# Conditioning rows loaded first, twelve tiles for modulation weights, and layer 0's five later modulation pieces on TensorE

## The chip, the core and the metric

The kernel runs on one core of a Trainium2 chip (trn2). The core has five instruction queues that run at the same time and wait for each other through semaphores: TensorE (PE in the profile; its weight loads are a row of their own, PEld), VectorE (DVE), ScalarE (ACT), GpSimd (POOL) and SyncE (SP), which issues nearly all the DMAs of this kernel. The metric is device microseconds of one execution. The kernel before took 1816.23 us (median of three runs, 1811.3 to 1817.52).

## The reference, cut to what matters

Two layers of a transformer trunk over 512 latent tokens and 256 context tokens, width 1024, all in float32. Every layer is modulated: a matrix product of the conditioning vector with `w_ada` gives six rows of 1024 numbers (shift, scale and gate for the attention half, the same for the FFN half), once for the latent tokens (`c`) and once for the context tokens (`c_ctx`).

```python
silu_c, silu_cc = silu(c), silu(c_ctx)
for l in range(2):
    mod   = silu_c  @ w_ada[l] + b_ada[l]        # (1024) @ (1024, 6*1024)
    mod_c = silu_cc @ w_ada[l] + b_ada[l]
    sh_a, sc_a, gt_a, sh_f, sc_f, gt_f = split(mod, 6)      # the same for mod_c
    h  = rms(x,  g_attn_pre) * (1 + sc_a)  + sh_a
    hc = rms(xc, g_attn_pre) * (1 + csc_a) + csh_a
    # one input projection for three head groups (MLA, differential, GQA)
    q, k, v of each group = project(h @ w_in[l]), project(hc @ w_in[l])
    x  = x  + gt_a  * rms(attention(...) @ w_out[l], g_attn_post)
    xc = xc + cgt_a * rms(...)                                # layer 0 only
    hf = rms(x, g_ffn_pre) * (1 + sc_f) + sh_f
    x  = x + gt_f * rms((silu(hf @ w_gate) * (hf @ w_up)) @ w_down, g_ffn_post)
    # and the same for xc in layer 0
```

## The kernel before

The work is cut into stages, each of which is a `Plan`: a list of steps, and for each step the engines that may do it with an estimated duration on each, the steps that it follows, the buffers that it takes, and a rank. When the kernel is built, `Plan.schedule` plays the list through: whenever an engine is free it takes the ready step with the lowest rank, and a step that several engines may do goes to the one that would end it first. The order that comes out is what each engine's queue holds; on the chip an engine runs its queue in that order and waits, in order, for whatever the next instruction needs. So every duration in the plan and every rank can move the order of all five queues.

The stages are, for the first layer: a start stage (the `with` block from line 839, tiles from pool `e0`), the rest of the input projection (from line 1003, which this text calls the projection stage), the attention, and then three plans for the output projection, the FFN's two first products and the down projection; the second layer has the same but for the start, which the first layer's last plan does for it.

Matrix products of the trunk are taken as three products of float32r parts (`mm3`, lines 433 to 437): a high part `wh` (cast by ACT at line 490) and a low part `wl` (the rest, line 431, on DVE or POOL) of each weight tile, and the same of the activations.

`ada` (line 504) computes one piece of the modulation: 512 of the 1024 columns of one of the six rows `v`. It loads eight tiles of `w_ada`, 128 by 512 each (256 KB), through a ring of tiles (`st` in the start stage, 7 of them; `ast` in the projection stage, 3 of them). There are three ways:

- `rows` and `columns`: DVE multiplies each tile by its column of `silu(c)` and adds it up (lines 527 and 529), once for each of the two streams (latent, context); then the sum is split into a high and a low part (`pair`) and TensorE adds up its 128 partitions. In `rows` two matmuls of 512 columns for each stream do that (line 545), and the row goes to DRAM (`mod_d`). In `columns` eight small matmuls for each stream do it (line 550) and leave the result in columns, where it is used.
- `pe`: TensorE multiplies each tile directly (line 519: 128 by 2 stationary, 512 float32 columns moving), eight matmuls for both streams at once, a copy and four small transposes (line 580) turn the row into columns.

In the start stage four pieces of layer 0 are done, two by `columns` and two by `pe` (`S_WAY`), and a fifth (`S_LATER`) by `rows`. In layer 0's projection stage the five pieces of `W_LATER[0]` are all done by `rows`, and so are the four pieces of `W_LATER[1]` in layer 1's, for one stream only. `mod_columns` (line 602) reads the FFN half's rows back from DRAM and turns them into columns (line 609). The conditioning vectors are loaded by `load_c` (lines 852, 853) into `crow`, turned by TensorE (line 856) and put through Silu by ACT (line 857) into `sc`, on which all of `ada` waits. `row_columns` loads the biases and gains (lines 629, 631).

`lean` is a flag of a plan: steps that DVE may do are then not offered to POOL. It is off in the projection stages. `KIND` chooses between two sets of estimated durations; set 1 is in force from layer 0's output projection to its down projection, and likewise in layer 1.

Of the kernel before, what the change touches and what calls it, by code (L numbers as in the profile page):

```python
# [59 lines left out]
D_ADA = (-2.8, 12, 15, 18.06, 27.82, 38)  # L60
W_ORDER = (('a', 'gq', 'v'), ('a', 'gq', 'v'))
W_MLA = (2, 2)
W_QB = (-23.02, 10.44)
W_MR = (30.2, 40.9)
W_ROPE = (23.16, -12.09)
W_GQN = (35.45, 8.86)
W_ADA = (-2.51, -2)
W_ADA_STEP = (3.15, 8)
W_BIAS = (1.57, 3.22)
R_KP = (41.16, 51.47)  # L70
O_BIAS = (0.99, 0.19)
O_Y = (((-23.8, -14.51), (-23.14, -6.37)), ((-23.71, -25.03), (-22.35, 6.93)))
O_FIN = (-1.05, -20.02)
O_W = (1.59, -10.71)
O_TAIL = ((1, 7), (1, 6))
O_GATE = (19.45, -11.16)
O_CH = ((13.48, 16.45), (9.41, 21.58))
O_CHS = (0.65, -3.01)
O_MOD = (-0.24, -11.23)
O_TR = (-3.5, -25.57)  # L80
O_W0 = (16.11, -1.02)
O_W1 = (36.25, 12)
F_BIAS = (0.27, 0.5)
F_ADA = (6.19, 0)
F_ADA_STEP = 4.5
F_W = (-11.64, -5.09)
# [7 lines left out]
D_CHS = (4.07, 1)  # L94
# [14 lines left out]
S_ROW = 0.4  # L109
S_CH = (149.71, 128.84, 43.28, -19.45)  # L110
# [25 lines left out]
class Plan:  # L136
# [7 lines left out]
    wrote, read, free, gone, over = {}, {}, {}, {}, 0.0  # L144

    @classmethod
    def reset(cls):
        cls.wrote, cls.read, cls.free, cls.gone, cls.over = {}, {}, {}, {}, 0.0
# [12 lines left out]
    def add(self, rank, ways, emit, after=(), takes=(), uses=(), lag=None, reads=(), writes=(), room=None):  # L161
# [3 lines left out]
        s = SimpleNamespace(rank=rank, n=len(self.steps), ways=ways, emit=emit, takes=takes, uses=(*takes, *uses),  # L165
# [51 lines left out]
    def schedule(self):  # L217
# [34 lines left out]
        while len(order) < len(self.steps):  # L252
            t = heapq.heappop(events)
            more = True
            while more:
                more = False
                for e in ready:
# [3 lines left out]
                    while ready[e]:  # L261
# [4 lines left out]
                        if s.at <= t and e == min(s.ways, key=lambda o: max(free[o], t) + s.ways[o] + (  # L266
                                self.bias if o == "dve" else 0)) and self.fits(s, t):
                            free[e] = t + s.ways[e]
                            self.start(s, free[e], e)
# [29 lines left out]
DMA = 0.66  # L299
# [6 lines left out]
KIND = [0]  # L306

# [40 lines left out]
def _body(nc, tc, es, I, out):  # L348
# [155 lines left out]
    def ada(plan, rank, l, v, c0, nstr, tiles, way="rows", late=False):  # L504
# [7 lines left out]
        for k in range(NK):  # L512
# [5 lines left out]
            if by_pe:  # L518
                last[0] = plan.add(rk, {"pe": 4 * c_mm(512) + 0.2}, lambda _, k=k, st=st: mm(
                    ps.tile[:2, :], lhsT=sc[:, :, k], rhs=st.tile[:, :512], start=(k == 0), stop=(k == NK - 1)),  # L520
                    [x, last.get(0, [])], [] if k else [ps], [st, ps] if k else [st], reads=["sc"])
                continue
            for s, a in enumerate(acc):
                def mac(_, s=s, a=a, k=k, st=st):
# [3 lines left out]
                    else:  # L528
# [3 lines left out]
                                   [] if k else [a], [st, a] if k else [st], reads=["sc"])  # L532
# [122 lines left out]
    def mean_inv(plan, rank, after, box):  # L655
# [5 lines left out]
        return plan.add(rank, {"pool": 0.46}, lambda _: power(box), [x])  # L661
# [79 lines left out]
    def residual(plan, rank, t, ps, gate, stage, dst, X, junk, after, mt_of):  # L741
# [12 lines left out]
        r = plan.add(rank, {"pool": 0.46}, lambda _: power(box), [plan.add(rank, {"dve": 0.13}, mean, a)])  # L754
# [84 lines left out]
    with ExitStack() as s0:  # L839
# [3 lines left out]
        plan = Plan({"m": 8, "st0": 7, "acc0": 4, "row0": 2, "pair": 1, "x": 6, "mt": 6, **RING}, ("m", "st0", "acc0", "row0"), 0.3)  # L843
        tiles = (held("st0", e0, [128, 512], 7), held("acc0", e0, [128, 512], 4), held("row0", e0, [128, 512], 2),
# [10 lines left out]
        x = plan.add(-50, {"sp": 2 * DMA}, load_c, lag=2.2)  # L855
        x = plan.add(-50, {"pe": 0.1}, lambda _: nc.tensor.transpose(psc.tile[:, 0:16], crow, ident[:16, :16]), [x], [psc])
        plan.add(-50, {"act": 1.5}, lambda _: A.activation(
# [12 lines left out]
        for i, (v, c0) in enumerate(S_LATER):  # L870
            ada(plan, 100 + i, 0, v, c0, 2, tiles)
# [3 lines left out]
    for l in range(DEPTH):  # L875
# [6 lines left out]
        with ExitStack() as sa:  # L882
# [50 lines left out]
            def rms_heads(rank, x, H, g, t, after, key):  # L933
# [20 lines left out]
                y = plan.add(rank, {"dve": c_vec(n) + 0.07}, sums, [y], (), [tmp])  # L954
                y = plan.add(rank, {"pool": 0.3 + 0.16 * H}, power, [y])
# [46 lines left out]

            sw = ExitStack()
# [4 lines left out]
            plan = Plan({"m": 8, "P": P_BUFS - nw - (1 if nw else 0), "qk": 4, "OT": 3, "sm": 2, "ast": 3, "pair": nw, **RING}, ("m", "P", "ast", "sm", "pair"), W_BIAS[l])  # L1008
# [1038 lines left out]
```

## Time and profile before

| | |
|---|---|
| median of three runs | 1816.23 us (1811.3 to 1817.52) |
| the profiled execution's own time | 1813.22 us |
| its span, first to last instruction | 1811.4 us |
| mean granted TensorE clock | 0.976 |
| instructions | 27865 |
| start stage, to the first matmul of part `a` | 0 to 94.7 us |
| layer 0's projection stage, to the first attention score | 94.7 to 235.8 us |

The profile is one execution. Its page gives busy time by engine and a picture in 40 slices; the trace behind it can be asked for groups of instructions by line, for who waited for whom, for the chain of work that ended last, for the timeline of one engine, and for the busy time of each engine in a stretch. Busy times of PE are modelled at their ends (a matmul of 512 columns is shown as 0.39 us and the next one starts 0.23 us after it), so the spacing of the starts is what a matmul costs when others follow it.

### The profile page before, as it was taken

The page shows a single profiled execution, that of the slowest core. Times are in us where ns is not written, and L with a number is a line of the kernel's source. Part 1 is how long each engine was busy: PE and PEld are TensorE (multiplying, and loading weights), DVE is VectorE, ACT ScalarE, POOL GpSimd, SP SyncE. Part 2 cuts the span into 40 slices and gives each one's busy share as a digit, 9 for nine tenths or more (in the row PEclk, how much of TensorE's full clock was granted, in tenths as well). Part 3 has the DMA queues.
Part 4 walks back from the last instruction along what each step waited for, and adds up shares of the span by engine and source line. Part 5 has one row for each costly group of instructions (what it writes and reads, how often), then busy time and mean ns, then how long its engine had stood idle before and what let it go on. Part 6 is the DMA issues. An engine that isn't in the chain of part 4 may idle for free.

```text
span 1811.4 us, 27865 instructions
## 1 busy us (share of the span) xinstructions
PE 1696.4 (94%) x9906; PEld 1494.3 (82%) x9906; DVE 1381.5 (76%) x1981; ACT 989.7 (55%) x2035; POOL 731.3 (40%) x789
## 2 busy tenths in 40 slices
PE   6888799999999999999999998988999979999998
PEld 2676588798888999999777888777898879999886
DVE  5869878887669899976788645558898799988444
ACT  3344278998586444443346564447996754555212
POOL 3576967788100000000000027886875127444212
PEclk8899899999999999999999999989999989999999
DMA  8245103100664544522888635402003644332532
GB/s 293 80 153 163 52 14 82 25 1 29 243 183 132 168 128 151 156 93 89 290 283 256 210 95 179 159 14 66 23 2 117 213 132 123 105 104 71 174 100 75
DMA packets 152636, 227.80 MB, mean 126 GB/s; under 512 B 14473, under 2 KB 86121, under 8 KB 152497
## 3 DMA queue, kind: packets, MB, share of 16 engines
q1 hardware_dynamic: 152496, 226.02, 39.4%
q8 instruction: 78, 1.28, 0.3%
q14 instruction: 62, 0.50, 0.1%
HBM read 197.58 MB, written 18.17 MB: 119 GB/s over the span
## 4 chain that ended last, share of the span: by engine, by line
PE 53%; DVE 14%; DMA 9%; ACT 9%; POOL 8%; issue 7%; SPq 0%; DVEq 0%; ACTq 0%; POOLq 0%
PE m L1742 25%; PE m L436 5%; PE m L435 5%; PE m L437 5%; PE s L1410 4%; DVE wl L431 3%; DMA st<-in_w_ffn_down 2%; PE m L1384 2%; PE m L1527 2%; DMA st<-in_w_out 2%; PE m L1468 2%; DVE P L529 2%; ACT wh L490 2%; ACT P L1423 1%; DMA st<-in_w_ada 1%
## 5 line engine op out<-in xcount | busy, mean ns | idle before, releaser
L1742 PE MATMUL m<-Y,wh 128*128 128x384 f32 (+1 forms) x1408 | 310.2, 311 | 6.0 <-ACT Y L419 4.9
L653 POOL TENSOR_TENSOR r<-v,mhalf 128x1 f32<-128x1 f32 x42 | 29.0, 692 | 687.4 <-DVE v L752 590.8
L490 ACT CAST wh<-st 128x1024 fp32r<-128x1024 f32 (+2 forms) x146 | 151.2, 1037 | 245.6 <-PE m L437 94.8
L431 DVE TENSOR_TENSOR wl<-st,wh 128x1024 fp32r<-128x1024 f32 (+1 forms) x124 | 164.5, 1327 | 107.8 <-ACT wh L490 107.2
L1742 PEld LDWEIGHTS m<-Y,wh 128*128 128x128 f32 x1408 | 239.4, 192 | 7.6 <-ACT Y L419 5.4
L1742 PE MATMUL m<-hT,wh 128*128 128x384 f32 (+1 forms) x1056 | 232.2, 311 | 3.6 <-ACT wh L490 3.6
L1742 PE MATMUL m<-Y,wl 128*128 128x384 f32 (+1 forms) x704 | 219.5, 312 | 6.5 <-DVE wl L431 6.5
L1742 PEld LDWEIGHTS m<-hT,wh 128*128 128x128 f32 x1056 | 178.6, 191 | 5.2 <-ACT wh L490 4.3
L1423 ACT ACTIVATE P<-s,nm 128x768 f32<-128x768 f32 (+1 forms) x200 | 164.4, 826 | 32.1 <-DVE nm L1416 12.5
L1416 DVE TENSOR_REDUCE nm<-s 128x1 f32<-128x768 f32 x160 | 151.1, 950 | 27.6 <-PE s L1410 23.2
L1742 PE MATMUL m<-hT,wl 128*128 128x384 f32 (+1 forms) x528 | 164.3, 311 | 2.3 <-DVE wl L431 2.3
L1692 ACT CAST wh<-X 128x1024 fp32r<-128x1024 f32 x82 | 86.2, 1053 | 113.2 <-PE m L1742 49.7
L435 PE MATMUL m<-wh,hT 128*128 128x512 f32 (+2 forms) x368 | 143.6, 390 | 0.6 <-POOL hT L417 0.4
L436 PE MATMUL m<-wl,hT 128*128 128x512 f32 (+2 forms) x368 | 141.5, 384 | 2.4 <-DVE wl L431 1.6
L437 PE MATMUL m<-wh,hT 128*128 128x512 f32 (+2 forms) x368 | 141.4, 384 | 2.2 <-POOL hT L431 1.7
L1742 PEld LDWEIGHTS m<-Y,wl 128*128 128x128 f32 x704 | 135.1, 192 | 7.9 <-DVE wl L431 7.9
L431 DVE TENSOR_TENSOR wl<-X,wh 128x1024 fp32r<-128x1024 f32 x82 | 107.3, 1309 | 14.2 <-ACT wh L1692 13.6
L436 PE MATMUL m<-wl,nr 128*128 128x512 f32 x264 | 103.4, 392 | 2.1 <-DVE wl L431 2.1
L435 PE MATMUL m<-wh,nr 128*128 128x512 f32 x264 | 103.8, 393 | 0.2 <-ACT wh L490 0.2
L1742 PEld LDWEIGHTS m<-hT,wl 128*128 128x128 f32 x528 | 100.8, 191 | 3.4 <-DVE wl L431 3.4
L437 PE MATMUL m<-wh,nr 128*128 128x512 f32 x264 | 103.0, 390 | 0.0
L529 DVE SCALAR_TENSOR_TENSOR P<-ast,sc,P 128x512 f32<-128x512 f32 x98 | 89.1, 949 | 15.5 <-DMA ast<-in_w_ada 15.2
(333 smaller groups left out, 4364.2 us busy)
## 6 DMA issues: line engine op xcount, KB each, us to landing
st<-in_w_ffn_down SPq DMA_DIRECT2D x66, 512.0 KB
st<-in_w_ada SPq DMA_DIRECT2D x88, 256.0 KB
ast<-in_w_ada SPq DMA_DIRECT2D x72, 256.0 KB
st<-in_w_out SPq DMA_DIRECT2D x32, 512.0 KB
X<-in_w_ffn_gate SPq DMA_DIRECT2D x22, 512.0 KB
X<-in_w_ffn_up SPq DMA_DIRECT2D x22, 512.0 KB
x<-in_w_ffn_up SPq DMA_DIRECT2D x22, 512.0 KB
x<-in_w_ffn_gate SPq DMA_DIRECT2D x22, 512.0 KB
```

The costliest lines, as they stand in the source:

```text
L431: by(e).tensor_tensor(out=out, in0=src, in1=h.bitcast(F32), op=ALU.subtract)
L435: mm(ps, lhsT=a[0], rhs=b[0], start=start, stop=False)
L436: mm(ps, lhsT=a[0], rhs=b[1], start=False, stop=False)
L437: mm(ps, lhsT=a[1], rhs=b[0], start=False, stop=stop)
L490: a = plan.add(rank, {"act": c_act(W) + 0.05}, lambda _: A.copy(out=part(0)[:, :W], in_=st.tile[:, :W]), [x], kept[:1], [st])
L529: V.scalar_tensor_tensor(out=a.tile[:, :512], in0=st.tile[:, :512], scalar=c, in1=a.tile[:, :512], op0=ALU.mult, op1=ALU.add)
L1384: mm(m.tile[0:64, :w], lhsT=U.vt(k + 6 - nk), rhs=kept.tile[:, k * w:(k + 1) * w], start=(k == 0), stop=(k == nk - 1))
L1410: mm(S.tile[:, o], lhsT=q[:, qt * 128:(qt + 1) * 128], rhs=k[:, ks], start=(i == 0), stop=(i == n))
L1416: V.tensor_reduce(out=nm[:, 0:1], in_=S.tile[:, :768], axis=AX.X, op=ALU.max, negate=True)
L1423: A.activation(out=P.tile[:, c], in_=S.tile[:, c], func=AF.Exp, bias=box["nm"][:, i:i + 1], scale=1.0, accum_out=r_()[:, t + i:t + i + 1])
L1692: a = plan.add(rank, {"act": c_act(1024) + 0.05}, lambda _: A.copy(out=kept[0].tile, in_=x.tile), after, kept[:1], [x])
L1742: mm(m.tile[:, :n], lhsT=ww, rhs=moving[y](z, k), start=bool(first) and k == 0 and t == 0, stop=k == 3 and t == 2, skip_group_check=not first)
```

## The change

The two conditioning rows get rank -200 in place of -50 and `row_columns` (`S_ROW`) -147.64 in place of 0.4, so SP issues them before all else. The start stage has 12 tiles for `w_ada` in place of 7. In layer 0's projection stage the five pieces are done by `pe` (`W_WAY[0]`), and the plan is lean; in layer 1's the four pieces are done by `columns`. `mod_columns` is no longer called in either. `KIND` is 1 in layer 0's projection stage too, with some estimated durations changed there (`either`), and a matmul of the `pe` way is planned at 0.45 us in place of 1.06 under set 1. Where set 1 is in force, the schedule lengthens a step on DVE and one on POOL by their overlap if they share operands' ports by a rule written into `add` (`shared`). Many ranks are new: most of the start stage's, some of the projection stage of layer 0, the output projections, the FFN of layer 1 and the down projection of layer 0.

```diff
-S_RANK = 4.71
-S_ADA = (-89.37, -104.7, -63.8, -23.26)
-S_W = (4.4, 70.86, -34.09, 21.27)
-S_X = (-23.02, -119.78, -29.53, 10.12, 31.11, 79.28)
-S_H = (21.12, 71.5, -0.39, 57.38, 59.34, 107.98)
+S_RANK = 18.42
+S_ADA = (-89.37, -93.77, -63.25, 11.71)
+S_W = (4.4, 57.56, -70.74, 21.27)
+S_X = (-40.27, -135.33, -29.53, 18.16, 31.11, 79.28)
+S_H = (21.12, 83.75, 31.93, 57.38, 59.34, 107.98)
...
+W_WAY = (('pe', 'pe', 'pe', 'pe', 'pe'), ('columns', 'columns', 'columns', 'columns'))
+W_LEAN = (True, False)
...
-W_ADA_STEP = (3.15, 8)
+W_ADA_STEP = (3.37, 8)
...
-O_W1 = (36.25, 12)
+O_W1 = (40.29, 17.37)
...
-F_W = (-11.64, -5.09)
+F_W = (-11.64, -21.22)
...
-D_CHS = (4.07, 1)
+D_CHS = (1.37, 1)
...
-S_ROW = 0.4
-S_CH = (149.71, 128.84, 43.28, -19.45)
+S_ROW = -147.64
+S_CH = (149.71, 128.84, 43.28, 7.44)
...
+        shared = shared or ("pool" in ways and ways["pool"] > 1.5 * ways.get("dve", 0.0))
...
+                            o = self.busy.get("pool" if e == "dve" else "dve")
+                            if KIND[0] and e in ("dve", "pool") and o is not None and o.end > t and (
+                                    s.shared or e == "pool") and (o.shared or o.on == "pool"):
+
+                                both = min(s.ways[e], o.end - t)
+                                free[e] += both
+                                o.end += both
...
+def either(a, b):
+    return (a, b)[KIND[0]]
...
-                last[0] = plan.add(rk, {"pe": 4 * c_mm(512) + 0.2}, lambda _, k=k, st=st: mm(
+                last[0] = plan.add(rk, {"pe": either(4 * c_mm(512) + 0.2, 0.45)}, lambda _, k=k, st=st: mm(
...
-        plan = Plan({"m": 8, "st0": 7, "acc0": 4, "row0": 2, "pair": 1, "x": 6, "mt": 6, **RING}, ("m", "st0", "acc0", "row0"), 0.3)
+        plan = Plan({"m": 8, "st0": 12, "acc0": 4, "row0": 2, "pair": 1, "x": 6, "mt": 6, **RING}, ("m", "st0", "acc0", "row0"), 0.3)
...
-        x = plan.add(-50, {"sp": 2 * DMA}, load_c, lag=2.2)
+        x = plan.add(-200, {"sp": 2 * DMA}, load_c, lag=2.2)
...
+            KIND[0] = 1 - l
...
                 for i, (v, c0) in enumerate(W_LATER[l]):
-                    ada(plan, W_ADA[l] + W_ADA_STEP[l] * i, l, v, c0, 2 - l, tiles)
-                mod_columns(plan, W_ADA[l] + W_ADA_STEP[l] * len(W_LATER[l]), l, 1, 2 - l, tiles[2])
+                    ada(plan, W_ADA[l] + W_ADA_STEP[l] * i, l, v, c0, 2 - l, tiles, W_WAY[l][i])
```

## Rows read from the trace of the kernel before

**Rows 1.** The profile page: busy time of each engine over the span, and the slices of PE.

```profile
PE 1696.4 (94%) x9906; PEld 1494.3 (82%) x9906; DVE 1381.5 (76%) x1981; ACT 989.7 (55%) x2035; POOL 731.3 (40%) x789
...
PE   6888799999999999999999998988999979999998
```

**Rows 2.** Busy time by stretch: start and end in us, its length, then for PE, PEld, DVE, ACT and POOL the busy time and the instructions, then the granted clock, the mean share of the DMA engines and GB/s. The first row is the whole projection stage of layer 0, the other two are holes in it.

```profile
94.70:235.80 141.10, 119.63 (x544) 97.38 (x543) 111.83 (x176) 54.64 (x143) 110.72 (x110) 0.94 0.39 119
123.00:129.90 6.90, 1.26 (x5) 0.39 (x4) 4.86 (x13) 4.98 (x20) 6.39 (x13) 0.75 0.46 133
197.40:207.40 10.00, 2.43 (x8) 1.26 (x9) 7.76 (x9) 2.81 (x4) 10.00 (x9) 0.71 0.26 79
```

**Rows 3.** Who waited for whom, PE alone, in the projection stage (94.7 to 235.8 us): us in total, times, the longest.

```profile
PE m L545 <- ACT pair L419: 8.0, 2, 4.5
PE m L545 <- POOL pair L431: 5.5, 4, 2.5
PE m L985 <- DVE ckTl L431: 2.4, 2, 1.7
PE m L545 <- DVE Vm L431: 1.5, 1, 1.5
PE m L985 <- ACT N L424: 1.4, 1, 1.4
PE m L609 <- DVE mql L971: 0.9, 1, 0.9
```

**Rows 4.** Timelines of PE and PEld: start in us, length, engine, line, operation, tiles, count, and the idle time before it. The weight loads of line 519 are shown because each starts when the matmul before it does.

```profile
31.53 1.05 PE L550 MATMUL m<-selr,pair 128*128 128x2 f32 x8
...
32.95 0.09 PEld L519 LDWEIGHTS m<-st,sc 128*2 128x2 f32 x1 [0.34 <-issue]
33.38 0.09 PEld L519 LDWEIGHTS m<-st,sc 128*2 128x2 f32 x1 [0.34 <-issue]
...
39.57 0.41 PE L580 MATMUL m<-ident,row 2*128 2x2 f32 x4 [0.92 <-ACT row L419]
...
129.88 0.63 PE L435 MATMUL m<-wh,hT 128*128 128x512 f32 x1
130.31 0.63 PE L436 MATMUL m<-wl,hT 128*128 128x512 f32 x1
...
137.44 0.39 PE L435 MATMUL m<-wh,hT 128*128 128x512 f32 x1
137.67 0.39 PE L436 MATMUL m<-wl,hT 128*128 128x512 f32 x1
```

**Rows 5.** Groups of instructions by line from 92 to 235 us, of PE, DVE and POOL: line, engine, operation, tiles, count, then busy us, mean ns of one, idle time before them and what ended it.

```profile
L545 PE MATMUL m<-pair,selr 128*2 128x512 f32 x20 | 8.6, 482 | 15.0 <-ACT pair L419 8.0 <-POOL pair L431 5.5 <-DVE Vm L431 1.5
...
L529 DVE SCALAR_TENSOR_TENSOR P<-ast,sc,P 128x512 f32<-128x512 f32 x70 | 59.4, 904 | 4.1 <-DMA ast<-in_w_ada 4.1
L431 DVE TENSOR_TENSOR wl<-st,wh 128x832 fp32r<-128x832 f32 (+1 forms) x5 | 6.1, 1225 | 3.5 <-ACT wh L490 3.4
L527 DVE TENSOR_SCALAR P<-ast,sc 128x512 f32<-128x512 f32 x10 | 5.8, 607 | 2.0 <-POOL pair L431 1.4 <-POOL kpn L916 0.6
...
L431 POOL TENSOR_TENSOR wl<-st,wh 128x1024 fp32r<-128x1024 f32 (+2 forms) x9 | 21.3, 2373 | 13.9 <-ACT wh L490 8.3 <-DMA ast<-in_w_ada 5.6
L431 POOL TENSOR_TENSOR pair<-P,pair 128x512 fp32r<-128x512 f32 x10 | 14.9, 1509 | 6.8 <-ACT pair L419 6.8
L951 POOL TENSOR_TENSOR r<-v,mhalf 128x8 f32<-128x8 f32 (+1 forms) x8 | 12.1, 1517 | 2.7 <-DVE v L946 2.7
```

**Rows 6.** Timeline of SP's queue at the start: what it issues, when, and for how long.

```profile
0.72 3.23 SPq L515 DMA_DIRECT2D st<-in_w_ada  x7
3.99 0.38 SPq L852 DMA_DIRECT2D crow<-in_c  x1
...
7.70 0.33 SPq L629 DMA_DIRECT2D row<-in_b_ada  x1
...
9.03 0.28 SPq L631 DMA_DIRECT2D row<-in_g_ffn_pre  x1
```

**Rows 7.** The chain of work that ended last, in order of time: start in us, length, what. Pieces of the start and, of the projection stage, two waits for a tile of `w_ada`.

```profile
4.41 5.00 DMA crow<-in_c_ctx
...
10.03 4.64 PE m L519 x6
...
142.19 2.90 DMA ast<-in_w_ada
...
198.94 3.48 DMA ast<-in_w_ada
```

**Rows 8.** Busy time by stretch, columns as in rows 2, in the start stage.

```profile
0.00:10.00 10.00, 0.26 (x1) 0.18 (x1) 0.49 (x6) 1.47 (x2) 0.68 (x6) 1.00 0.82 280
10.00:15.00 5.00, 4.97 (x8) 0.85 (x9) 1.34 (x5) 3.45 (x6) 3.00 (x5) 1.00 0.56 194
25.00:50.00 25.00, 21.98 (x74) 10.75 (x74) 23.01 (x35) 9.60 (x25) 12.00 (x10) 0.74 0.93 313
50.00:75.00 25.00, 20.93 (x81) 16.31 (x82) 23.87 (x28) 12.52 (x24) 13.72 (x9) 0.80 0.29 87
```

**Rows 9.** Groups of PE from 1060 to 1200 us, layer 1's projection stage.

```profile
L545 PE MATMUL m<-pair,selr 128*2 128x512 f32 x8 | 3.3, 452 | 3.5 <-POOL pair L431 2.3 <-ACT pair L419 1.2
```

**Rows 10.** Who waited for whom, PE alone, from 1380 to 1540 us: layer 1's output projection and the start of its FFN.

```profile
PE m L1742 <- DVE wl L431: 7.8, 10, 3.0
```

More of the change, by code (lines that the diff above doesn't have):

```diff
@@ L142 @@
     LAG = {"pe": 0.2, "act": 0.14, "dve": 0.13, "pool": 0.07, "sp": 0.15}
-    wrote, read, free, gone, over = {}, {}, {}, {}, 0.0
+    wrote, read, free, gone, over, busy = {}, {}, {}, {}, 0.0, {}
     @classmethod
     def reset(cls):
-        cls.wrote, cls.read, cls.free, cls.gone, cls.over = {}, {}, {}, {}, 0.0
+        cls.wrote, cls.read, cls.free, cls.gone, cls.over, cls.busy = {}, {}, {}, {}, 0.0, {}
     def __init__(self, bufs, loose=(), bias=0.0, new=(), lean=False):
@@ L159, in __init__, with add @@
         self.live = {tag: [] for tag in bufs}
-    def add(self, rank, ways, emit, after=(), takes=(), uses=(), lag=None, reads=(), writes=(), room=None):
+    def add(self, rank, ways, emit, after=(), takes=(), uses=(), lag=None, reads=(), writes=(), room=None,
+            shared=False):
         if self.lean and "dve" in ways:
             ways = {e: c for e, c in ways.items() if e != "pool"}
-        s = SimpleNamespace(rank=rank, n=len(self.steps), ways=ways, emit=emit, takes=takes, uses=(*takes, *uses),
+        shared = shared or ("pool" in ways and ways["pool"] > 1.5 * ways.get("dve", 0.0))
+        s = SimpleNamespace(shared=shared, rank=rank, n=len(self.steps), ways=ways, emit=emit, takes=takes, uses=(*takes, *uses),
                             lag=lag, end=None, on=None, nexts=[], plan=self, need={}, room=room or {})
@@ L268, in schedule @@
                             free[e] = t + s.ways[e]
+                            o = self.busy.get("pool" if e == "dve" else "dve")
[4 more added lines that the diff above has]
+                                o.end += both
+                                if free[o.on] < o.end:
+                                    free[o.on] = o.end
+                                for h in o.uses:
+                                    h.end = max(h.end, o.end + self.LAG[o.on])
+                                heapq.heappush(events, o.end)
+                                heapq.heappush(events, o.end + self.LAG[o.on])
+                                for y in o.nexts:
+                                    y.at = max(y.at, self.seen(o, y))
+                                    heapq.heappush(events, y.at)
+                            self.busy[e] = s
                             self.start(s, free[e], e)
@@ L870, in _body @@
         for i, (v, c0) in enumerate(S_LATER):
-            ada(plan, 100 + i, 0, v, c0, 2, tiles)
+            ada(plan, 100 + i, 0, v, c0, 2, tiles, "rows")
         plan.add(70, {"sp": 2 * DMA}, lambda _: (dma(out=ropeS, in_=I["rope_s"]), dma(out=ropeL, in_=I["rope_l"])))
@@ L1007, in _body @@
             h_pair = slots("pair", attw, [128, 2, 512], nw, F32R)
-            plan = Plan({"m": 8, "P": P_BUFS - nw - (1 if nw else 0), "qk": 4, "OT": 3, "sm": 2, "ast": 3, "pair": nw, **RING}, ("m", "P", "ast", "sm", "pair"), W_BIAS[l])
+            plan = Plan({"m": 8, "P": P_BUFS - nw - (1 if nw else 0), "qk": 4, "OT": 3, "sm": 2, "ast": 3, "pair": nw, **RING}, ("m", "P", "ast", "sm", "pair"), W_BIAS[l], lean=W_LEAN[l])
             toks = list(range(NT))
@@ L1998, in _body @@
             run(plan)
-            KIND[0] = 0
             if not last:
```

55 lines of the change are left out of this document (28 added, 27 removed).

## The prediction

> **What bounds the kernel now.** I read the page first, then the stretches, then the waits, then the timelines. The page says that TensorE is the busy engine, 94% of the span, and the picture in slices says where it is not: in the first five slices, 226 us with the digits 6, 8, 8, 8 and 7, and in a few later ones [rows 1]. So the whole is a TensorE kernel with a few stages in which TensorE waits. The change touches two of these: the start (0 to 94.7 us) and layer 0's projection stage (94.7 to 235.8 us).
>
> For the projection stage, look at the three stretches [rows 2]. PE is shown busy 119.6 of 141.1 us, and the two holes (123.0 to 129.9 and 197.4 to 207.4) hold 13.2 us in which it does next to nothing; the granted clock over them is 0.75 and 0.71, so part of them and of what follows runs at 1.2 GHz. The waits name the cause [rows 3]: PE's line 545, the `rows` reduction, stands in PE's queue and waits 8.0 + 5.5 + 1.5 = 15.0 us for ACT, POOL and DVE to hand over the split sums (`pair`). Everything queued behind it on PE, the projection matmuls, waits too. Behind `pair` stands DVE: 70 multiply-adds of 904 ns and 10 multiplies of 607 ns, 65.2 us of work [rows 5], in a stage in which DVE is busy 111.8 and POOL 110.7 us of 141.1. So here the stage is bound by PE's work plus its in-order waits on a loaded DVE and POOL.
>
> What the stage costs PE if it never waits: spacing of starts is 0.23 us for a 512-column float32r matmul at full clock and 0.43 at half clock [rows 4].
>
> **The change part by part.** *Removed from PE, projection stage.* The 15.0 us of waits at line 545 [rows 3, 5]; the 20 matmuls themselves at 0.23 = 4.6; line 609's wait and transpose, 1.0, since `mod_columns` goes. After the two holes PE runs at half clock for a while: from 129.88 on its matmuls start 0.43 apart [rows 4], 19 matmuls in the two places, 19 x 0.20 = 3.8. Sum 24.4 us.
>
> *Added to PE there.* 40 matmuls of line 519. Their weight loads start 0.43 us apart at full clock (32.95, 33.38) [rows 4]: 40 x 0.43 = 17.2. Four of the five pieces need four transposes, 0.41 us for a set [rows 4]: 1.6. Sum 18.8, all of it on PE's path, since PE has no slack here. Net so far -5.6 us.
>
> *DVE and POOL there.* DVE loses the 65.2 us of multiply-adds. Being lean, it takes over what POOL did but for its powers (line 951, 12.1 us, and a few more) and a little else; `pair` (14.9 us on POOL) falls away. That is about 75 of POOL's 110.7 us, and DVE does the same in about half: a low part `wl` takes 1225 ns on DVE against 2373 on POOL [rows 5], so about 38 us. DVE ends near 111.8 - 65 + 38 = 85 us of some 134, one engine in place of two, but with room. I cost the move at nothing; if that cover fails it costs a wait of line 985's kind (up to 2.4 us for a place). The other way, the waits of the MLA transposes for DVE and ACT, 2.4 + 1.4 us, with small ones beside them about 5.4 in all [rows 3], should shrink: I take half, -2.7.
>
> *New waits on PE.* Line 519 waits in PE's queue for its tile, and the projection matmuls wait behind it. There are three tiles; a lone load takes 2.90 us from issue to use, one behind other loads 3.48, and in the crowded start one took 5.00 [rows 7]. The plan has 2.2 us after the issue. Between nothing and (5.0 - 2.9) x 13 groups of three = 27 us; the stage moves 119 GB/s of DMA against 313 in the start [rows 2, 8], so I go by the lone load: nothing. The transposes of line 580 wait for a copy by ACT, 0.92 us where seen [rows 4]; between 0 and 4 x 0.92 = 3.7, I take 1.3, since other matmuls can stand between. A PSUM bank is now held while eight tiles come in, not only for the reduction; no row shows a price, and I put it between 0 and the 2.4 us of the longest small wait, at 0.
>
> Projection stage: -5.6 - 2.7 + 1.3 = -7.0 us. Its ends: all small waits gone, -11.0; tile waits as in the start, +21.
>
> *The start.* The conditioning row is issued at 3.99 us, behind seven tiles [rows 6], lands 5.00 us after the second issue, and the first modulation matmul starts at 10.03 [rows 7]. Issued first, at 0.72, landing after a lone 2.90, it would be there some 5 us sooner. But three row loads (7.70 to 9.3) and one `x` tile now also stand ahead of the first tile of `w_ada` in SP's queue: about 1.0 + 2.0 + 0.6 us, so that tile is issued near 4.3 in place of 0.72 and lands near 7.2. The first matmul comes 2.8 us earlier, not 5. The transfers lose 3.6 us at the front and gain the hole in 10 to 15, where the DMA share is 0.56 (2.2 us), since twelve tiles let SP run ahead [rows 8]. What bounds the rest is DVE, busy 23.0 and 23.9 of 25 us from 25 to 75 [rows 8]; it starts its first sums as soon as the first `columns` piece lands, and fewer other loads stand ahead of that piece now. Ends: +1.5 (transfers alone) and -8 (DVE starts sooner by the whole of it and some half-clock time goes as well: 0.74 and 0.80 in these two stretches). I take -4.
>
> *Layer 1's projection stage.* `columns` takes eight matmuls for a piece and stream, 1.05 us for a set, 4.2 in all [rows 4], for eight of line 545, 1.8 (0.23 each, [rows 9]). The waits for `pair` (3.5 us) stay. `mod_columns` goes, 0.2. Net +2.2; I take +2, between 0 and +4.
>
> *New orders elsewhere.* The output projections, FFN and down projection get other ranks and another rule for DVE and POOL steps; no instruction is added. What they can win is PE's waits there, the largest group of which is 7.8 us for low parts in layer 1 [rows 10]; `F_W` moves those loads ahead. Between -7.8 and as much given back; I take a quarter, -2.
>
> **Sum:** -7 - 4 + 2 - 2 = -11 us. The profiled execution took 1813.2, which becomes 1802; the median of the runs shown is 3.0 above it, so 1805.
>
> The Trainium skill's Perfetto Trace Analysis, in Identifying the Most-Contended Engine, says to find the engine with the highest occupancy and work on that one first. By the page that is PE, and the change loads PE further; were the advice the whole story here, the sum would be positive (last rival). The trace disagrees for this stage: PE's waits there are 15.0 us on one line. The same page warns that matmul busy time is a poor measure, and that regimes differ.
>
> **The rivals.**
> *PE packed:* all small waits go too (-11.0), the start wins 8, the FFN orders win 8, layer 1 costs 2: -25, 1791. For it: DVE and POOL lose over 60 us of work between them. Against: some waits are for transfers.
> *Given back:* the start stays bound by transfers (0), the new orders win nothing, the small waits stay: -5.6 + 1.3 + 2 = -2, so 1814, no change that can be told. For it: DMA share 0.93 from 25 to 50 us.
> *Tiles late on PE (slower):* in the projection stage line 519 takes the place of line 545 as the waiter. With three tiles each group of three waits for its load. At 1.7 us a group over what the plan allows, 13 x 1.7 = 22 us: -11 + 22 = +11, 1827. It decides from 11 / 13 = 0.85 us a group; the lone load shows 0, the load behind others 0.6, the crowded start 2.1 [rows 7].
> *PE bound throughout (slower):* no wait comes back, because other steps of DVE are late instead, and PE pays 18.8 + 4.2 for new matmuls less 6.6 for old ones: +16, 1832. The holes [rows 2] speak against it. This is what that page's advice would lead one to expect.
> That the change does not do what it says concerns only the twelve tiles: with the transfers the limit they may stay empty. That is the case given back.
>
> **How the numbers follow.** Forecast (1797 to 1811) 0.45; PE packed 0.20; given back 0.17; tiles late 0.12; PE bound 0.06. A measurement of this kernel can tell about 0.3%, 5.4 us, from no change. Faster is the forecast and PE packed, 0.65; same 0.17; slower 0.18. The range reaches from 1788, a little past PE packed, to 1825, which takes in most of the bound for late tiles.
>
> **What would show it.** In the changed profile (lines numbered as before): no line 545 in layer 0's projection stage, 72 matmuls of line 519 in the first 240 us, spaced 0.43 us; PE's waits there short and for DMA or ACT; that stage about 134 us long, DVE busy some 85 us of it; the first line 519 near 7 us; the `a` part starting near 91 us. Wrong would be: waits of line 519 for `ast` over 11 us in sum; the stage over 141 us; the low parts on DVE late for the matmuls; later stages longer by more than 2 us apart from layer 1's projection.

## The result and the profile after

The changed kernel takes 1841.35 us (median of 4 runs, 1839.76 to 1841.51) against 1815.47 for the kernel before in the same session: a ratio of 1.0144, 95% interval 1.0124 to 1.0163. It is slower by some 26 us, where 1805 us had been forecast. The profiled executions have spans of 1839.7 and 1811.4 us, 28.2 apart before rounding.

In the lines of the changed kernel 461 to 463 are the projection matmuls (before 435 to 437), 545 the float32 matmul of the `pe` way (519), 571 the `rows` reduction (545), 606 the transposes (580), 1437 the attention scores (1410), 1450 the exponentials (1423).

The page answers to [rows 1]. TensorE has 41 us more work at the same share, and GpSimd loses 193 us:

```profile
PE 1737.7 (94%) x10004; PEld 1505.0 (82%) x10004; DVE 1354.8 (74%) x2134; ACT 971.4 (53%) x1979; POOL 538.7 (29%) x606
...
PE   7799999898998999999999999979999979999998
```

**Where the 28.2 us are.** I cut both spans at the same instructions: in each layer the first matmul of part `a` (416 columns) and the first and the last score matmul. The first three lines hold more than the whole difference; the last three give 4.1 us back.

| Stage, us | before | after |
|---|---|---|
| start, to part `a` | 94.7 | 97.1 |
| projection, layer 0 | 141.1 | 153.2 |
| attention, layer 0 | 201.9 | 219.7 |
| its output, FFN, down projection, to `a` of layer 1 | 648.7 | 648.2 |
| projection and attention, layer 1 | 290.4 | 290.2 |
| its output, FFN, down projection | 434.6 | 431.2 |

So 12.1 us are lost in the projection and 17.8 in attention 0, whose program the change does not touch at all. The rows of the score matmuls show where attention starts and ends (first and last start, the numbers ahead of the shape); before, then after:

```profile
L1410 PE MATMUL s<-EX,gq x160: 274/284/507, 353.4 to 437.7; 128*128 128x256 f32 x96, 128*128 128x512 f32 x64
...
L1410 PE MATMUL s<-mkh,mqh x40: 277/286/498, 235.8 to 281.6; 96*128 96x256 f32 x24, 96*128 96x512 f32 x16
```

```profile
L1437 PE MATMUL s<-EX,gq x160: 274/284/504, 377.3 to 470.1; 128*128 128x256 f32 x96, 128*128 128x512 f32 x64
...
L1437 PE MATMUL s<-mkh,mqh x40: 277/386/792, 250.3 to 301.3; 96*128 96x256 f32 x24, 96*128 96x512 f32 x16
```

**The projection stage** answers to [rows 2]. Stretches of after, columns as there; the first is the stage, then come the handover to attention and attention 0 as a whole:

```profile
97.00:250.00 153.00, 150.81 (x620) 98.38 (x618) 81.07 (x250) 36.77 (x85) 20.95 (x19) 1.00 0.36 109
250.30:470.00 219.70, 203.68 (x1421) 179.25 (x1422) 168.09 (x302) 184.71 (x470) 150.46 (x172) 0.96 0.10 24
...
245.00:250.00 5.00, 2.88 (x13) 2.06 (x11) 4.89 (x30) 2.75 (x12) 2.10 (x3) 0.99 0.00 0
250.00:255.00 5.00, 4.67 (x16) 4.09 (x17) 3.44 (x15) 0.00 (x0) 1.41 (x2) 0.50 0.00 0
```

The holes are gone, the clock stays at full, VectorE has 81 us to do and GpSimd 21. TensorE is busy 150.8 of 153.0 us. All the waits of [rows 3] went, one new wait of 2.4 us came at the end (`Vg`, below), and the stage is still longer. The groups say why; the first row is the forty float32 calls:

```profile
L545 PE MATMUL m<-ast,sc 128*2 128x512 f32 x80 | 38.2, 592 | 0.1
...
L457 DVE TENSOR_TENSOR wl<-st,wh 128x1024 fp32r<-128x1024 f32 x8 | 9.7, 1217 | 2.2 <-ACT wh L516 2.2
```

Five pieces of eight calls are 40, and the row counts 80. The weight loads of that line in the same stage:

```profile
121.11 0.09 PEld L545 LDWEIGHTS m<-ast,sc 128*2 128x2 f32 x1 [0.34 <-issue]
121.54 0.09 PEld L545 LDWEIGHTS m<-ast,sc 128*2 128x2 f32 x1 [0.34 <-issue]
121.97 0.09 PEld L545 LDWEIGHTS m<-ast,sc 128*2 128x2 f32 x1 [0.34 <-issue]
```

The spacing is 0.43 us, as in [rows 4], but it is that of instructions: a float32 call of 512 columns is two of them, 0.86 us. The trace of before said so too, in a row whose count I did not set against the code, the one of line 519 in its start stage, where two pieces make 16 calls:

```profile
L519 PE MATMUL m<-st,sc x32: 592/592/1062, 10.0 to 36.6; 128*2 128x512 f32 x32
```

**The start** answers to [rows 6 to 8]. SP now issues the conditioning rows at 0.72 us and the first float32 matmul starts at 5.24 in place of 10.03, 4.8 us sooner where 2.8 were forecast; part `a` still starts 2.4 us later.

```profile
0.72 0.40 SPq L878 DMA_DIRECT2D crow<-in_c  x1
...
2.56 8.04 SPq L541 DMA_DIRECT2D st<-in_w_ada  x14
```

The gain is lost near the end of the stage, by the mechanism that the prediction saw in the projection. The fifth piece's `rows` reduction stands in TensorE's queue until GpSimd has copied the sum that VectorE finishes late. TensorE waits 6.4 us for it, and its next matmuls start 0.43 us apart (half clock) until 89.2 us. Before, the longest wait for `pair` in the start stage was 1.0 us.

```profile
83.17 0.59 PE L571 MATMUL m<-pair,selr 128*2 128x512 f32 x1 [6.38 <-POOL pair L443]
84.52 0.58 PE L571 MATMUL m<-pair,selr 128*2 128x512 f32 x1 [0.76 <-POOL pair L457]
84.90 0.63 PE L461 MATMUL m<-wh,hT 128*128 128x512 f32 x1
```

**Attention 0.** Who waited for whom on TensorE, before and after:

```profile
PE s L1410 <- ACT P L1423: 4.3, 8, 1.1
PE m L1384 <- ACT PTf L419: 1.3, 1, 1.3
```

```profile
PE s L1437 <- ACT P L1450: 8.7, 13, 1.8
PE s L1437 <- DVE Vg L457: 2.4, 1, 2.4
PE m L1411 <- ACT PTf L445: 1.8, 2, 1.3
PE m L1336 <- DVE gq L997: 1.5, 1, 1.5
```

The scores wait twice as long for exponentials, 13 times in place of 8, though the same steps are to be done. Their order is another: of TensorE's some 1,400 records in this stage only 79% can be matched in one common sequence of both traces (operations, tile names and shapes compared in order; below, "agreement").

### The profile page after: what moved, and what is told of

Same layout as the page of the kernel before. It is cut to its first block, busy times and chain, and to the rows that moved or that the text cites. A ratio compares the mean times of both kernels' runs of the same rounds, so it can differ in the third digit from the quotient of the medians.

```text
span 1839.7 us, 27879 instructions
## 1 busy us (share of the span) xinstructions
PE 1737.7 (94%) x10004; PEld 1505.0 (82%) x10004; DVE 1354.8 (74%) x2134; ACT 971.4 (53%) x1979; POOL 538.7 (29%) x606
## 4 chain that ended last, share of the span: by engine, by line
PE 55%; DVE 8%; ACT 7%; POOL 5%; issue 5%; DMA 4%; SPq 0%; ACTq 0%; POOLq 0%; DVEq 0%
PE m L1769 27%; PE m L461 6%; PE m L462 6%; PE m L463 6%; PE s L1437 3%; PE m L1554 2%; ACT P L1450 2%; DMA st<-in_w_out 2%; DVE nm L1443 2%; PE m L1495 2%; DVE wl L457 2%; PE m L1411 1%; DMA st<-in_w_ffn_down 1%; ACT wh L516 1%; DVE PT L457 1%
## 5 line engine op out<-in xcount | busy, mean ns | idle before, releaser
L516 ACT CAST wh<-st 128x1024 fp32r<-128x1024 f32 (+2 forms) x146 | 151.3, 1037 | 207.0 <-PE m L463 85.6
L457 DVE TENSOR_TENSOR wl<-st,wh 128x1024 fp32r<-128x1024 f32 (+2 forms) x133 | 172.6, 1299 | 103.9 <-ACT wh L516 103.4
L1443 DVE TENSOR_REDUCE nm<-s 128x1 f32<-128x768 f32 x160 | 151.3, 951 | 42.4 <-PE s L1437 34.3
L457 DVE TENSOR_TENSOR wl<-X,wh 128x1024 fp32r<-128x1024 f32 x82 | 102.3, 1249 | 23.2 <-ACT wh L1719 22.5
L461 PEld LDWEIGHTS m<-wh,hT 128*128 128x128 f32 x368 | 71.1, 193 | 32.4 <-issue 17.3
```

The lines of the kernel that those rows point to most:

```text
L457: by(e).tensor_tensor(out=out, in0=src, in1=h.bitcast(F32), op=ALU.subtract)
L461: mm(ps, lhsT=a[0], rhs=b[0], start=start, stop=False)
L516: a = plan.add(rank, {"act": c_act(W) + 0.05}, lambda _: A.copy(out=part(0)[:, :W], in_=st.tile[:, :W]), [x], kept[:1], [st])
L1443: V.tensor_reduce(out=nm[:, 0:1], in_=S.tile[:, :768], axis=AX.X, op=ALU.max, negate=True)
```

## The experiments

First theory: the projection is bound by TensorE, and the float32 calls at twice the assumed price are the excess; attention 0 is slow because the planner, which carries its engines' times from one plan into the next, wrote another list for it. Rivals: late tiles, or a single lean VectorE, set the projection; attention 0 suffers from work really left over, not from its list.

**Rows again in the changed kernel**

```
-W_WAY = (('pe', 'pe', 'pe', 'pe', 'pe'), ('columns', 'columns', 'columns', 'columns'))
+W_WAY = (('rows', 'rows', 'rows', 'rows', 'rows'), ('columns', 'columns', 'columns', 'columns'))
...
+if 'rows' in W_WAY[l]:
+    mod_columns(plan, W_ADA[l] + W_ADA_STEP[l] * len(W_LATER[l]), l, 1, 2 - l, tiles[2])
```

> The changed kernel with one part undone: layer 0's five pieces by rows again (and mod_columns for them); the lean plan, the start and all new orders stay. Theory 1 (a float32 matmul of 512 columns is two instructions of 0.43 us, so the five pieces cost TensorE 34.4 us and not 17.2, and the stage is bound by TensorE): 36 us of TensorE's work go and 4.6 come back with 0 to 15 us of waits, so the projection stage falls from 153.2 us to between 122 and 137. Rival (the stage is long because one DVE does the work of two engines): it stays at 150 or more. For the attention, which took 219.7 us and 201.9 before: theory 2a (its order is wrong because the plan thought TensorE free 17 us too early) says 200 to 206 again; rival 2b (the attention's order follows from lean and from where the engines stand, whatever the planned cost) says 212 or more. In total about 1808 by 1 and 2a, 1822 by 1 and 2b, 1840 by the rival.

1836.53 us, ratio 1.0119 (1.0102 to 1.0136). The stage took 149.2 us, so my first theory missed (122 to 137), and the rival came close (150 or more): with the sums back and GpSimd kept off, VectorE does two engines' work.

```profile
97.10:246.30 149.20, 118.45 (x545) 97.47 (x544) 127.15 (x294) 48.01 (x120) 21.09 (x19) 0.89 0.37 112
```

```profile
PE m L571 <- ACT pair L445: 16.5, 2, 9.3
```

TensorE needs no more than before (118 us), VectorE 127, and TensorE waits. With the sums in the stage the lean rule seems to cost time (149.2 us against the 141.1 of before), but ranks and planned durations differ too, so its own share is not shown. Attention 0 took 217.2 us, with the changed kernel's list, record for record on TensorE.

**The `pe` way alone in the kernel before**

```
-    ada(plan, W_ADA[l] + W_ADA_STEP[l] * i, l, v, c0, 2 - l, tiles)
-mod_columns(plan, W_ADA[l] + W_ADA_STEP[l] * len(W_LATER[l]), l, 1, 2 - l, tiles[2])
+    ada(plan, W_ADA[l] + W_ADA_STEP[l] * i, l, v, c0, 2 - l, tiles, ('pe', 'rows')[l])
+if l:
+    mod_columns(plan, W_ADA[l] + W_ADA_STEP[l] * len(W_LATER[l]), l, 1, 2 - l, tiles[2])
```

> The kernel before with one part alone: layer 0's five pieces by pe (planned at 1.06 us a matmul), no mod_columns there. Theory 1: 141.1 - 24.4 for what goes + 36.0 for what comes - 2.7 gives a projection stage of 150 us. Rival, late tiles: float32 matmuls wait for their tiles, 10 us or more in sum, and the stage is 160 or more. Rival, the prediction's own price of 0.43 us: 134. For the attention: theory 2a says 200 to 206 us, since the planned cost is near the true one; 2b gives no reason for 201.9 to stay. In total 1825 by theory 1, 1835 by late tiles, 1808 by the prediction's price.

1830.74 us, 1.0088 (1.0073 to 1.0104). The stage is longer still, 159.0 us. TensorE is busy 151 of them without the new start, the lean rule and the new ranks, about as in the changed kernel, so that load is the way's own. Here the tiles come late besides, which they do not in the changed kernel:

```profile
95.10:254.00 158.90, 151.23 (x619) 99.42 (x617) 44.46 (x100) 51.59 (x139) 74.94 (x103) 0.98 0.34 105
...
PE m L519 <- DMA ast<-in_w_ada: 6.6, 4, 5.5
```

Its attention list is that of before, record for record, and attention 0 takes 207.3, so the `pe` way as such does not turn the list.

**The planner told 0.88 us for a call in place of 0.45**

```
-{"pe": either(4 * c_mm(512) + 0.2, 0.45)}
+{"pe": either(4 * c_mm(512) + 0.2, 0.88)}
```

> The changed kernel with one number changed: a float32 matmul of the pe way is planned at 0.88 us in place of 0.45 in layer 0's projection stage. Same instructions, another order. Theory 1: that stage stays within 4 us of 153.2, since TensorE is bound there by its work. Theory 2a: the attention's order is right again and it takes 200 to 206 us, in total about 1825. Rival 2b: it takes 212 to 222 us, in total about 1840.

1833.38 us, 1.0094 (1.0077 to 1.0110): the projection 149.5 us behind a start of 99.1 (together 1.8 us less than in the changed kernel), attention 0 217.2, its list still the changed kernel's. The wrong planned cost is not what turned it.

**Half the columns in seven of eight calls**

```
-lambda _, k=k, st=st: mm(ps.tile[:2, :], lhsT=sc[:, :, k], rhs=st.tile[:, :512], ...)
+lambda _, k=k, st=st, n=(256 if k and KIND[0] else 512): mm(ps.tile[:2, :n], lhsT=sc[:, :, k], rhs=st.tile[:, :n], ...)
```

> The changed kernel, same order of all queues, but seven of the eight matmuls of each of layer 0's five later pieces take 256 of the 512 columns: half of these modulation columns lack seven eighths of their sum. Theory 1: 35 x 0.43 = 15 us of TensorE's time go and the projection stage falls from 153.2 to 138 us. Rival, late tiles: TensorE waits for the tiles instead and the stage falls by less than 5. Theory 2a (the plan's TensorE and the chip's agree now): the attention falls from 219.7 to between 200 and 207, in total about 1810. Rival 2b (the order itself is bad): it stays within 4 of 219.7, in total about 1826.

1825.28 us, 1.0052 (1.0036 to 1.0068). The stage falls by 14.3 us to 138.9 (35 x 2 x 0.21 = 15), with TensorE still busy nearly throughout. So the price of the calls is on the path at its full length:

```profile
97.30:236.20 138.90, 135.59 (x619) 98.21 (x617) 81.18 (x250) 36.55 (x85) 20.96 (x19) 1.00 0.39 120
```

This is also the stage at about the price that the forecast assumed, 138.9 where it said 134. Attention 0 stays at 217.4 behind a shorter stage: theory 2a missed, rival 2b held.

**The attention list put back, and turned in the kernel before.** The planner's state at the start of attention 0 is overwritten, in the changed kernel with VectorE 2 us behind TensorE, in the kernel before with 8.8:

```
+if l == 0:
+    Plan.free.update({e: Plan.free["pe"] + d for e, d in back})
...
+back = (("act", 1.14), ("dve", 2.0), ("pool", 10.48), ("sp", -14.03))      # put back, kernel after
+back = (("act", 3.05), ("dve", 8.82), ("pool", 7.89), ("sp", -14.77))      # turned, kernel before
```

> The kernel after, with one thing changed: when the planner starts the list of attention 0 it is told that VectorE comes free 2 us behind TensorE (as in the plan of before, 1.55) in place of 8.8 us. Nothing of the projection changes; the list of attention 0 turns back to that of before, all but some 3% of its TensorE entries. Theory (the list that follows from the handed-over state is the slow thing): attention 0 takes 203 to 208 us in place of 219.7, projection 0 stays at 153 and the whole comes to 1825 to 1832 us. Rival (the work that the engines really have left over from the longer projection slows attention, whatever its order): attention 0 stays at 216 to 221 and the whole at 1838 to 1843.

> The kernel before, its plan of attention 0 started as if VectorE came free 8.8 us behind TensorE (as in the plan of after) in place of 1.55; projection 0 and all else as before. Its attention list agrees with that of after in 97% of the entries. Theory (the list is the slow thing): attention 0 takes 212 to 219 us in place of 201.9 and the whole 1825 to 1833. Rival (real work left over): attention 0 stays within 3 us of 201.9 and the whole within 5 us of before.

Put back: 1828.32 us, 1.0076 (1.0061 to 1.0091); attention 0 takes 208.9 in place of 219.7, a little above the expected range, agreement with before 99%. Turned: 1828.65 us, 1.0089 (1.0068 to 1.0110); attention 0 takes 216.3 in place of 201.9, with after's list, record for record, and the edit touches nothing else in that kernel. The waits follow the list; first the kernel after with the list put back, then the kernel before with it turned:

```profile
PE s L1439 <- ACT P L1452: 4.1, 8, 0.9
PE s L1439 <- DVE Vg L457: 2.4, 1, 2.4
```

```profile
PE s L1412 <- ACT P L1425: 8.5, 12, 1.8
```

The list is worth 11 to 14 us. Over all the profiles, one execution each, attention 0 takes 216.3 to 219.7 us in the five kernels with the new list and 201.9 to 211.2 in the nine with before's (agreement 97% or more). The other part, 7.0 us with the list put back, is about what the granted clock took: 0.96 in place of 1.00 over attention 0 is some 8 us of 208.9. Work left over, the rival's cause, shows in one place, the wait for `Vg`, which stands ahead of the first score and counts to the projection. The turned kernel's 14.4 us hold some 3 to 4 us of clock too (0.98), so that the list itself is worth about 11 us both ways, as an estimate from these clocks. Attention 0 as a whole, before, with the list put back, and turned:

```profile
235.80:437.70 201.90, 192.62 (x1408) 170.18 (x1406) 166.43 (x293) 183.99 (x472) 155.53 (x191) 1.00 0.11 27
```

```profile
250.50:459.40 208.90, 199.81 (x1406) 176.83 (x1407) 166.84 (x302) 183.37 (x468) 146.98 (x166) 0.96 0.11 26
```

```profile
235.20:451.50 216.30, 199.40 (x1423) 175.36 (x1422) 167.55 (x293) 185.42 (x475) 159.26 (x197) 0.98 0.10 25
```

How late each score matmul starts against the kernel before, by its number among the 360 of the stage, shows both parts:

| Score matmul | after | list put back | before, turned | start alone | both repairs |
|---|---|---|---|---|---|
| 0 | 14.5 | 14.7 | -0.7 | 0.0 | 3.0 |
| 32 | 20.4 | 20.0 | 2.9 | 3.8 | 4.6 |
| 144 | 19.7 | 20.1 | 1.9 | 3.8 | 4.7 |
| 160 | 24.4 | 20.1 | 6.6 | 3.9 | 4.7 |
| 288 | 22.8 | 21.7 | 4.2 | 3.9 | 4.7 |
| 304 | 29.5 | 21.7 | 10.8 | 3.9 | 4.7 |
| 352 | 31.2 | 21.7 | 12.6 | 3.9 | 4.7 |

Kernels with before's list run in step with it for 200 us, but for a jump within the first 32 and, in some, one of 1.6. Those with the other list lose 5 to 7 us at two places more, 144 to 160 and 288 to 304.

**The start alone, and the late orders alone.** Against the kernel before, and against the kernel after with before's `S_` and `W_` ranks:

```
-x = plan.add(-50, {"sp": 2 * DMA}, load_c, lag=2.2)
+x = plan.add(-200, {"sp": 2 * DMA}, load_c, lag=2.2)
-tiles = (held("st0", e0, [128, 512], 7), ...
+tiles = (held("st0", e0, [128, 512], 12), ...
...
+S_RANK = 18.42     # and S_ADA, S_W, S_X, S_H, S_ROW, S_CH
```

```
-W_WAY = (('pe', 'pe', 'pe', 'pe', 'pe'), ...
+W_WAY = (('rows', 'rows', 'rows', 'rows', 'rows'), ...
-W_LEAN = (True, False)
+W_LEAN = (False, False)
-KIND[0] = 1 - l
+KIND[0] = 0
...                 # loads, seven tiles and mod_columns as before
```

> The kernel before with the start of the change alone: conditioning rows first, twelve tiles for the modulation weights, the new ranks of the start; its attention list stays that of before. If the start of the change is what its rows say in the kernel after (97.1 for 94.7), the start takes 97 and the whole is 2 to 3 us over before. Rival: the 2.4 us are the price of the projection that follows in the kernel after (its weights and modulation loads are queued earlier), and alone the start is no longer than 94.7.

> The kernel after with before's start and before's projection of layer 0 (five pieces by rows, one by columns, no lean rule, the old costs and ranks); what is left of the change is the orders from the output stage on and the fourth piece of layer 1. Its attention 0 follows before's list but for 3%. From the stages of the kernel after (projection 1 -2.6, attention 1 +2.5, output and feed-forward 1 -2.8, the rest -1) it should come out 2 to 6 us under before, 1809 to 1813, with the four stages up to attention 0 within 4 us of before. Rival: those gains come from the shifted start of the later stages and are not there alone: within 2 us of before.

Start alone: 1818.90 us, 1.0029 (1.0015 to 1.0043), slower by a little. Part `a` starts 1.7 us later, behind the same wait of 6.4 us for `pair`, and attention at 235.8, as before. So the start does not give the 4 us forecast. All eight profiles with the new start have that wait (6.4 us) and reach part `a` at 96.4 to 99.7 us; the six with the old one wait at most 2.0 us for `pair` there and reach it at 93.9 to 96.5. The 3.8 us of this kernel's profile arise in the first 32 score matmuls, where one hole stands and the clock sinks behind it; whether the start is their cause is not shown:

```profile
ACT P L1423 <- POOL N L916: 2.8, 1, 2.8
```

```profile
245.00:250.00 5.00, 4.81 (x27) 4.33 (x25) 2.80 (x5) 3.79 (x11) 3.85 (x6) 0.69 0.04 10
```

Late orders alone: 1812.62 us, 0.9993 (0.9982 to 1.0005), no difference that can be told for the whole; this kernel keeps layer 1's pieces by columns as well, and +2 and -2 had been forecast for the two. Cut into stages, the profiles tell them apart. The last stage takes 434.6 to 436.4 us in the four kernels with the old late orders and 429.6 to 431.6 in the ten with the new, so these win more than the 2 us forecast; layer 1's projection and attention take 288.0 to 290.4 and 289.4 to 293.8 (means 289.5 and 291.6), the +2 that was forecast. The wait that the forecast named, for low parts in layer 1, is not what went: 7.8 us before [rows 10], 8.7 in this kernel.

**One and two pieces on TensorE.** In the last kernel, attention's start told as before, the first piece, or the first and the last, go the `pe` way:

```
-W_WAY = (('rows', 'rows', 'rows', 'rows', 'rows'), ...
+W_WAY = (('perow', 'rows', 'rows', 'rows', 'rows'), ...
-by_pe, rows = way == "pe", way == "rows"
+by_pe, rows = way in ("pe", "perow"), way in ("rows", "perow")
...
```

> Late orders alone as in e8, and in layer 0's projection one of the five pieces (the first) on TensorE, its eight float32 calls planned at 0.88 us, no lean rule, conditions' rows kept for it; the planner is handed before's state at attention 0, so that its list stays. If every microsecond of TensorE in that stage is on the path: +6.9 us for 16 instructions of 0.43, less 3.0 us of waits, 0.9 of matmuls and 0.8 of half clock for the piece by rows: the stage 2 us over e8's 142.8, the whole 1812 to 1817. Rival (VectorE and GpSimd, 111 us busy each, set the stage, and TensorE's holes take the calls up): the stage shrinks by 4 to 7 us to 136 to 139, the whole 1803 to 1810.

> As e9 with the first and the last of the five pieces on TensorE. If TensorE is on the path throughout: the stage 4 to 5 us over e8's 142.8, the whole 1815 to 1820. Rival (VectorE and GpSimd set it): 8 to 13 us less, 130 to 135, the whole 1799 to 1806. Between them: TensorE's 121 us busy grow by 12 to 133, so that 135 is the least that the stage can take.

1820.48 us, 1.0041 (1.0026 to 1.0056), and 1825.47 us, 1.0067 (1.0052 to 1.0082). The stage takes 147.6 and 144.8 us (start and stage together 241.5 and 241.3, for 237.5 without). The totals are above every range that was expected. The holes do not take the calls up: TensorE's waits at the reduction go down from 15.2 us to 10.3 with one piece, and the calls add 6.9 of work and a wait for a tile. In the kernel with one piece:

```profile
PE m L545 <- DMA ast<-in_w_ada: 4.6, 1, 4.6
PE m L571 <- POOL pair L443: 3.6, 1, 3.6
```

A mixture pays for both ways; neither of the two shares tried is a gain.

**Both repairs at once, and the lean rule off.** The first joins the two edits above, half columns and the list put back; the second is the list put back and

```
-W_LEAN = (True, False)
+W_LEAN = (False, False)
```

> The kernel after with both repairs at once: seven of eight float32 calls of layer 0's projection take 256 columns (half of the columns of those five pieces lack seven eighths of their sum, as in the run with half columns), and the planner starts attention 0 with VectorE free 2 us behind TensorE. Theory (two causes that add): projection 0 at 138 to 140 us, attention 0 at 205 to 210, the whole at 1811 to 1817, so that the change would have been level with before, not 10 us faster, had the price been what the forecast took. Rival (they do not add: with the shorter stage the attention is handed another state, or the gain is taken back later): 1820 or more.

> The kernel after with the lean rule of layer 0's projection off, so that GpSimd may take elementwise steps there, and the planner's start of attention 0 as in the run with the order put back. If TensorE bounds the stage (151 of 153 us busy) the projection stays within 2 us of 153.1 and the whole within 4 us of that run's 1826. Rival (VectorE alone is what ends the stage late and leaves the hole at the handover): projection 0 and attention 0 together fall by 5 us or more.

Both repairs: 1809.33 us, 0.9981 (0.9966 to 0.9996), with the projection at 139.1 and attention 0 at 203.5. The causes add: against the kernel before, half columns alone take 0.92 points off the ratio, the list alone 0.68, both 1.63. Lean off: 1828.51 us, 1.0087 (1.0059 to 1.0114), projection 151.3, attention 0 211.2, together 362.5 for 362.0 with the rule on. So with the sums away the rule cost nothing in sum, but by two parts that cancel: without it the wait for `Vg` is gone and TensorE is busy the whole stage (151.3 us), and attention 0 then has one wait of 6.3 us for exponentials (its list agrees with before's in 97%). No version that computes the whole beat the kernel before.

## Why the prediction was wrong

**The step that failed** is "40 x 0.43 = 17.2". The spacing in [rows 4] was right and was taken for a call's; it is an instruction's, and a call is two. The sign "72 matmuls of line 519" has the same slip: it adds 32 instructions (16 calls) to 40 calls, and the trace has 112 instructions. At full clock the forty calls take 34.4 us. With that the stage's sum is -7.0 + 17.2 = +10.2 us; measured were +12.1, of which 2.4 are one wait for `Vg` at the stage's end. The rest held as a sum. The waits and the half clock that went can be worked out from the stage of after: 153.2, less that wait, 34.4 of calls and 1.6 of transposes, and with 4.6 of removed matmuls, is 119.4 us of work, so 141.1 held 21.7 us of them; 15.0 + 1.0 + 3.8 + 2.7 = 22.5 had been counted. Term by term it is partly luck: the small waits went whole (5.4, not 2.7), the transposes' wait of 1.3 did not come, and about 3.5 us that went the other way have no row to show them. The 85 us of VectorE were 81; its lean load, costed at nothing, cost the one wait for `Vg`, the 2.4 us that the prediction named for the case that its cover fails. A piece costs TensorE 6.9 us by its calls; by rows it had cost 0.9 and its share of the waits, 3.0.

The Trainium skill's FP8 and Floating Point Precision, in TensorE Precision Notes, says "True FP32: 4 passes through PE array". This trace agrees: a call takes 0.86 us against 0.23 for a float32r matmul of the same columns [rows 4], 3.7 times. The prediction did not weigh that page.

**What was not in the prediction at all** is attention 0. "New orders elsewhere" was meant for stages whose ranks change. Attention's do not, but its list is written from the state in which the projection's plan ends, and turned with it: 14.4 us in the kernel before (turned), 10.8 in the kernel after (put back). The other 7.0 us are the first 32 score matmuls (5.3) and the jump of 1.6, both in stretches of half clock.

**The rivals.** Late tiles were not it: 0.4 us on one call in the changed kernel, 6.6 with the `pe` way alone. "PE bound throughout" had the sign and nearly the size (1832), but by a mechanism that did not come: it let the waits return. They went, and the calls cost double. The start (-4) was wrong in sign: the first matmul came sooner than forecast, and the 6.4 us wait for the fifth piece's `pair`, which the sum did not hold, took it back. The late orders (-2) and layer 1 (+2) came about as forecast by stage, the orders larger and not by the wait named. With the price near the one assumed (19.7 us for 17.2) and before's list the kernel came out about level with before (0.998), not 11 us faster.

TensorE is busy 98.6% of the stage after the change. The sums came from an engine with 29 us idle of 141.1 and went to the one with 21 [rows 2] and took 36 there. The prediction set aside here the Trainium skill's Perfetto Trace Analysis, in Identifying the Most-Contended Engine. By the matmuls' busy time (119.6 us against VectorE's 111.8) its advice had the right sign. But the Trainium skill has TensorE judged there by MFU or its weight loads, not by that time; the weight loads were busy 97.4 us, less than VectorE [rows 2], so the advice does not settle this stage.

**What stays open.** Which difference of the handed-over state decides on the list: it turned neither with the planned cost of a call nor with the way alone, and the two runs that moved it set four engines' times at once, VectorE's the furthest (1.55 us behind TensorE in the plan of before, 8.8 in that of after). The jump in the first 32 score matmuls was not taken away by itself, and nothing here shows what decides how long the clock stays down. Which wait the late orders shorten in the last stage was not traced.

## What to carry to other kernels

Divide the count of a row by the calls in the code before using its spacing as a price: a float32 call may be two instructions. Where one greedy planner writes the lists of stages in turn, a change in one stage can rewrite the next; compare the order of the untouched stages first, and keep their starting state fixed when testing an edit. Work that is moved onto the busiest engine must be cheaper there than the waits that it ends; here its holes did not take it up by themselves. A reduction that waits in the queue of the engine that bounds the kernel can take back what an earlier start gives.

## What the runs showed of the hardware

The same instructions behind the same wait can get a different clock. With the list put back and with both repairs TensorE stands 2.44 us for `Vg` at the handover, after matmuls at full clock, and then does the same scores. In the first the granted clock was 0.54, 0.50 and 0.59 in the 15 us that follow (1.2 GHz is 0.5), and 5.3 us were lost by the 32nd score matmul:

```profile
250.00:255.00 5.00, 4.50 (x15) 3.93 (x16) 3.44 (x16) 0.00 (x0) 1.41 (x2) 0.54 0.00 0
255.00:260.00 5.00, 4.18 (x17) 3.58 (x16) 3.03 (x8) 3.19 (x8) 0.00 (x0) 0.50 0.00 0
260.00:265.00 5.00, 5.00 (x25) 4.72 (x25) 1.31 (x2) 3.54 (x10) 2.62 (x4) 0.59 0.00 0
```

In the second it was 0.66 for 5 us and then full, and 1.5 us were lost by that matmul:

```profile
238.60:243.60 5.00, 4.73 (x21) 4.16 (x21) 3.85 (x16) 0.44 (x2) 1.41 (x2) 0.66 0.00 0
243.60:248.60 5.00, 3.81 (x28) 3.37 (x27) 3.69 (x9) 4.39 (x14) 0.35 (x1) 1.00 0.00 0
```

The jump of 1.6 us is of that kind too: the kernel with the late orders alone has before's list to the last entry, and a clock of 0.74 from 328 to 333 us, where the same scores ran at 1.00 in the kernel before. TensorE's longest stand in the 15 us ahead was 0.9 us in both. Before, then the late orders alone:

```profile
326.00:331.00 5.00, 5.00 (x41) 4.37 (x40) 3.19 (x8) 4.91 (x17) 4.28 (x5) 1.00 0.00 0
```

```profile
328.00:333.00 5.00, 5.00 (x32) 4.42 (x31) 2.41 (x6) 3.40 (x14) 3.23 (x3) 0.74 0.00 0
```
